# Two neighbouring rows of x per partition, and other row blocks of weights, in a sliding-window matmul that streams its weights

## Chip, cores, metric

One core of one Trainium2 chip. The metric is device time in microseconds, taken outside the profile; the span in a profile, from the first to the last instruction of the program, is some 2 us shorter (180.1 against 182.17 us in the kernel before).

## The reference

```python
B, S, D, W = 4, 4096, 4096, 64
x: (4, 4096, 4096) float32,  w: (4096, 4096) float32,  offsets: (4,) int64
for b in range(B):
    o = int(offsets[b])
    results.append(x[b, o:o+W] @ w)        # 64 rows of x against all of w
return np.stack(results)                   # (4, 64, 4096) float32
```

There are 256 rows of x in all, so w (67 MB) is read once and dominates the bytes.

## The kernel before

Weights come from HBM in float32 and are cast to fp16 by the DMA on the way (the profile has 71.3 MB read from HBM, while the DMA packets, as written and with the 4.19 MB of stores, are 40.97 MB). They arrive in row blocks of r k tiles: partition p holds rows p·r to p·r+r-1 of the block, so one piece of a transfer is r·16 KB long in HBM. The blocks live in a ring of three buffers, and a transfer into a buffer waits for the matmuls that read it (GpSimd waited 108.1 us in all for PE before it issued blocks). x is read at run-time offsets, 64 rows a batch, transposed on TensorE (PE) with an identity, and used as the stationary operand. Two groups g of 128 rows are formed.

```python
blocks = [(0, 1), (1, 1), (2, 4), (6, 4), (10, 4), (14, 4), (18, 4), (22, 3), (25, 2), (27, 1)]
x16 = [x_pool.tile([P, D], fp16, name=f"xrow{g}") for g in range(G)]     # one row a partition
...
nc.gpsimd.dma_start(out=w_one[1][:], in_=w[P : 2 * P, :])                # k tile 1, then x
make_identity(nc, identity[:])
for b in range(B):
    g, m = divmod(b, 2)
    o = nc.values_load(...)
    nc.gpsimd.dma_start(out=x16[g][m * WIN : (m + 1) * WIN, :], in_=x[b][bass.ds(o, WIN), :])
for k0, r in blocks[2:]:
    if free < r:
        t = wc_pool.tile([P, R_MAX * N], fp16, name="wc", tag="wc")      # ring of 3
        free = R_MAX
    ...
    nc.gpsimd.dma_start(out=t[:, base : base + r * N],
        in_=w[k0 * P : (k0 + r) * P, :].rearrange("(p r) n -> p (r n)", r=r))
...                                             # transposes of g = 0, then of g = 1
whole_rows([0, 1], True)                        # matmuls of 2 k tiles, copied to acc
for k0, r in blocks[2:-n_join]:
    whole_rows(range(k0, k0 + r))               # matmuls of a block, added to acc
...                                             # k 25 to 31 by column halves, with their stores
out_rows = out.rearrange("b m n -> (b m) n")
```

K tile 0 comes in float32 over the queue of SyncE and is cast by ScalarE. K tiles 28 to 31 (the tail) come in column pieces, so that the last half of the output can be finished soon after the last piece lands (landing at 169.33 us, PE's last matmul at 171.67). The first half of the output is stored from GpSimd's queue, the second from those of ScalarE and SyncE.

Of the kernel before, what the change touches and what calls it, by code (L numbers as in the profile page):

```python
# [10 lines left out]
def kernel(  # L11
# [7 lines left out]
    nc = tc.nc  # L19
    fp32 = mybir.dt.float32  # L20
    fp16 = mybir.dt.float16

    B, S, D = x.shape
    _, N = w.shape
    WIN = out.shape[1]
    P = 128
    NT = 512
    NG = N // 2
    n_k = D // P
    n_sub = NG // NT  # L30
    G = B // 2
    POOL = mybir.EngineType.Pool


    blocks = [(0, 1), (1, 1), (2, 4), (6, 4), (10, 4), (14, 4), (18, 4), (22, 3), (25, 2), (27, 1)]
    n_join = 2
    k_tail = 28
    n_fine = 2
# [3 lines left out]
    x_pool = ctx.enter_context(tc.tile_pool(name="xp", bufs=1))  # L42
    wc_pool = ctx.enter_context(tc.tile_pool(name="wc", bufs=3))
    w1_pool = ctx.enter_context(tc.tile_pool(name="w1", bufs=1))
# [2 lines left out]

    identity = const_pool.tile([P, P], fp16, name="identity")
    off_t = const_pool.tile([1, B], mybir.dt.int64, name="off_t")
    x16 = [x_pool.tile([P, D], fp16, name=f"xrow{g}") for g in range(G)]  # L50
    xT = [x_pool.tile([P, D], fp16, name=f"xT{g}") for g in range(G)]
    w_one = [w1_pool.tile([P, N], fp16, name=f"w1_{i}") for i in range(2)]
    tmp = [acc_pool.tile([P, 2 * NT], fp32, name=f"tmp{i}") for i in range(G)]
    acc = [acc_pool.tile([P, N], fp32, name=f"acc{g}") for g in range(G)]
    pairs = [psum_pool.tile([P, 2 * NT], fp32, name=f"banks{t}") for t in range(4)]

    def banks(b, n=1):
        return pairs[b // 2][:, b % 2 * NT : (b % 2 + n) * NT]
# [4 lines left out]
    w0_32 = acc[1]  # L63
    nc.sync.dma_start(out=w0_32[:, :NG], in_=w[0:P, :NG])
    nc.scalar.dma_start(out=off_t[:], in_=offsets[None, :])
    nc.sync.dma_start(out=w0_32[:, NG:], in_=w[0:P, NG:])
    nc.scalar.copy(out=w_one[0][:, :NG], in_=w0_32[:, :NG])  # L67
    nc.scalar.copy(out=w_one[0][:, NG:], in_=w0_32[:, NG:])  # L68
    off_i32 = off_t.bitcast(mybir.dt.int32)

    nc.gpsimd.dma_start(out=w_one[1][:], in_=w[P : 2 * P, :])  # L71
    make_identity(nc, identity[:])
    for b in range(B):
        g, m = divmod(b, 2)
        o = nc.values_load(  # L75
            off_i32[0:1, 2 * b : 2 * b + 1],
            engines=[POOL],
            min_val=0,
            max_val=S - WIN,
            skip_runtime_bounds_check_because="offsets are drawn below S - WIN",  # L80
        )
        nc.gpsimd.dma_start(  # L82
            out=x16[g][m * WIN : (m + 1) * WIN, :],
            in_=x[b][bass.ds(o, WIN), :],
        )


    src = {
        0: lambda a, e: w_one[0][:, a:e],
        1: lambda a, e: w_one[1][:, a:e],  # L90
    }
    free = 0
    for k0, r in blocks[2:]:
        if free < r:
            t = wc_pool.tile([P, R_MAX * N], fp16, name="wc", tag="wc")
            free = R_MAX
        base = (R_MAX - free) * N
        free -= r
        nc.gpsimd.dma_start(  # L99
            out=t[:, base : base + r * N],  # L100
            in_=w[k0 * P : (k0 + r) * P, :].rearrange("(p r) n -> p (r n)", r=r),
        )
        for q in range(r):
            src[k0 + q] = lambda a, e, t=t, c=base + q * N: t[:, c + a : c + e]


    tail = {}
# [5 lines left out]
    t = wc_pool.tile([P, R_MAX * N], fp16, name="wc", tag="wc")  # L113
    pos = 0
    for ng, st in zip(order, (steps, fine_steps)):
        for ki, n, c0, c1 in st:
            wd = c1 - c0
            nc.gpsimd.dma_start(  # L118
                out=t[:, pos : pos + n * wd].rearrange("p (t n) -> p t n", t=n),
                in_=w[ki * P : (ki + n) * P, ng * NG + c0 : ng * NG + c1].rearrange(  # L120
                    "(t p) n -> p t n", p=P
                ),
            )
            for q in range(n):
                for j in range(wd // NT):
                    a = pos + q * wd + j * NT
# [3 lines left out]
    def x_cols(g, kt):  # L130
        for k0, r in blocks:
            if k0 <= kt < k0 + r:
                a = k0 * P + kt - k0
                return x16[g][:, a : a + r * (P - 1) + 1 : r]
        return x16[g][:, kt * P : (kt + 1) * P]

    for g in range(G):
        for t in range(4):
            for i in range(8):
                nc.tensor.matmul(  # L140
                    out=pairs[t][:, i * P : (i + 1) * P],
                    lhsT=x_cols(g, 8 * t + i),
                    rhs=identity[:],
                    start=True,
                    stop=True,
                )
            dst = xT[g][:, 2 * t * NT : 2 * (t + 1) * NT]
            if t % 2 == 0:
                nc.vector.tensor_copy(out=dst, in_=pairs[t][:])  # L149
            else:  # L150
                nc.scalar.copy(out=dst, in_=pairs[t][:])  # L151

    def mm(bank, g, kt, rhs, start, stop):
        nc.tensor.matmul(  # L154
            out=banks(bank),
            lhsT=xT[g][:, kt * P : (kt + 1) * P],
            rhs=rhs,
            start=start,
            stop=stop,
        )  # L160

    def add_out(bank, n, g, c):
        dst = acc[g][:, c * NT : (c + n) * NT]
        nc.vector.tensor_add(out=dst, in0=dst, in1=banks(bank, n))  # L164
# [3 lines left out]
    def whole_rows(kts, first=False):  # L168
        nonlocal n_pair
        for g in range(G):  # L170
            for c in range(0, 2 * n_sub, 2):
                b0 = n_pair % 4 * 2
                n_pair += 1
                for j in range(2):
                    for i, kt in enumerate(kts):
                        rhs = src[kt]((c + j) * NT, (c + j + 1) * NT)
                        mm(b0 + j, g, kt, rhs, i == 0, i == len(kts) - 1)
                dst = acc[g][:, c * NT : (c + 2) * NT]
                if not first:
                    add_out(b0, 2, g, c)  # L180
                elif c % 4 == 0:
                    nc.vector.tensor_copy(out=dst, in_=banks(b0, 2))  # L182
                else:
                    nc.scalar.copy(out=dst, in_=banks(b0, 2))  # L184

    whole_rows([0, 1], True)
    for k0, r in blocks[2:-n_join]:
        whole_rows(range(k0, k0 + r))
    join = range(blocks[-n_join][0], k_tail)
# [3 lines left out]
        rhs = src[ki](c * NT, (c + 1) * NT) if ki < k_tail else tail[(ki, c)]  # L193
        mm(4 * g + j, g, ki, rhs, start, stop)

    out_rows = out.rearrange("b m n -> (b m) n")

    def store(eng, g, c0, c1, cuts=(0, P)):
        for a, e in zip(cuts, cuts[1:]):
            eng.dma_start(out=out_rows[g * P + a : g * P + e, c0:c1], in_=acc[g][a:e, c0:c1])  # L200

    def columns(ng, kts):
        for ki in kts:
# [14 lines left out]
    for g in range(G):  # L218
        store(nc.gpsimd, g, ng * NG, (ng + 1) * NG)
# [8 lines left out]
    for h in range(2):  # L228
        js = range(h * n_sub // 2, (h + 1) * n_sub // 2)
        for ki in range(k_fine, n_k):  # L230
            for g in range(G):
                for j in js:
                    tail_mm(ki, g, ng, j, False, ki == n_k - 1)
        for g in range(G):
            add_out(4 * g + js[0], 2, g, ng * n_sub + js[0])
            c0 = ng * NG + h * NG // 2
            store(q[g], g, c0, c0 + NG // 2)
# [30 lines left out]
```

## Time and profile before

| | before |
|---|---|
| median of 3 runs | 182.17 us (182.05 to 182.88) |
| span in the profile | 180.1 us |
| PE busy | 128.2 us, 71% |
| DMA queues, share of 16 engines | 100% |
| read from HBM / written | 71.3 / 4.19 MB |

How to read it: PE is TensorE's matmuls and PEld its loads of the stationary operand, DVE is VectorE, ACT is ScalarE, POOL is GpSimd; a transfer "lands" when the trace reports its end. The digits of a row in the 40 slices are tenths of a slice of 4.5 us in which that engine was busy. The DMA share is the mean over 16 engines. A stretch's share can pass 1 a little (1.16 from 13.3 to 23.1 us), as the query books a piece's time whole where it starts. The rows themselves stand in the prediction.

### The profile page before, as it was taken

To read this page: it belongs to the slowest core of one execution; us is meant where nothing else is said; L and a number is where in the kernel's file an instruction comes from. 1 tells how busy PE (TensorE), PEld (TensorE's weight loads), DVE (VectorE), ACT (ScalarE), POOL (GpSimd) and SP (SyncE) were. 2 spreads that over 40 slices of the span, in tenths; PEclk is the share of its full clock that TensorE was granted. 3 is DMA by queue.
4 is the path that set the end of the run, shared out by engine and by line. 5 is a ranking of instruction groups with operands and counts; after the bars stand their busy time and mean duration, and the time that the engine had idled before them with its cause. 6 is when DMAs were issued, how large, how long until landed. Compare 5 with 4: busy or idle time off the path is not lost.

```text
span 180.1 us, 1403 instructions
## 1 busy us (share of the span) xinstructions
PE 128.2 (71%) x576; PEld 57.3 (32%) x576; DVE 82.2 (46%) x68; ACT 16.9 (9%) x15; POOL 12.7 (7%) x27
## 2 busy tenths in 40 slices
PE   0000789104999499938996599949999999999910
PEld 0000764001344134413442134414444444443400
DVE  0000566200276427642566036733778975407560
ACT  2422346200000000000000000000000004004000
POOL 4600000000000100010001000020007100000200
PEclk9999999855599969996999569987999999999995
DMA  5999979999998899999989999999999999999996
GB/s 187 313 260 213 286 160 211 236 233 226 233 233 175 182 233 233 236 218 233 204 175 218 233 233 220 222 193 202 229 206 215 198 211 213 214 214 207 338 412 241
DMA packets 4151, 40.97 MB, mean 227 GB/s; under 512 B 434, under 2 KB 434, under 8 KB 2226
## 3 DMA queue, kind: packets, MB, share of 16 engines
q0 software_dynamic: 3280, 36.70, 93.5%
q1 hardware_dynamic: 576, 3.15, 4.6%
q10 hardware_dynamic: 290, 1.05, 1.5%
q8 instruction: 4, 0.07, 0.1%
q14 instruction: 1, 0.01, 0.0%
HBM read 71.30 MB, written 4.19 MB: 419 GB/s over the span
## 4 chain that ended last, share of the span: by engine, by line
DMA 43%; PE 43%; issue 4%; DVE 2%; another core or an unknown queue 1%; POOLq 1%; DVEq 1%; POOL 1%
DMA wc<-in_w_dram 43%; PE banks L154 43%; DVE acc L164 2%; DVEq L263 1%; POOLq L75 1%; POOL xrow L82 0%; POOL identity masks.py:197 0%; POOLq L82 0%; POOL w L71 0%; POOLq masks.py:199 0%; DVEq L164 0%; POOLq L252 0%
## 5 line engine op out<-in xcount | busy, mean ns | idle before, releaser
L154 PE MATMUL banks<-wc,xT 128*128 128x512 f16 x480 | 115.8, 405 | 23.6 <-DMA wc<-in_w_dram 23.3
L164 DVE TENSOR_TENSOR acc<-acc,banks 128x1024 f32<-128x1024 f32 x56 | 67.9, 1221 | 69.0 <-PE banks L154 68.4
L154 PEld LDWEIGHTS <-xT 128*128 128x128 f16 x512 | 52.3, 103 | 93.9 <-DMA wc<-in_w_dram 26.4
L140 PE MATMUL banks<-identity,xrow 128*128 128x128 f16 x64 | 5.3, 261 | 19.9 <-DMA xrow<-in_x_dram 19.9
L209 ACT COPY tmp<-banks 128x1024 f32<-128x1024 f32 x4 | 3.9, 1016 | 128.2 <-PE banks L154 128.2
L149 DVE CAST xT<-banks 128x1024 f16<-128x1024 f32 x4 | 4.8, 1222 | 21.5 <-PE banks L140 21.5
L99 POOL DMA_DIRECT2D wc<-in_w_dram x8 | 4.3, 539 | 108.1 <-PE banks L154 108.1
L140 PEld LDWEIGHTS <-xrow 128*128 128x128 f16 x64 | 5.1, 127 | 20.0 <-issue 20.0
L154 PE MATMUL banks<-w,xT 128*128 128x512 f16 x32 | 7.1, 379 | 0.0
L182 DVE COPY acc<-banks 128x1024 f32<-128x1024 f32 x4 | 4.9, 1225 | 1.6 <-PE banks L154 1.6
L118 POOL DMA_DIRECT2D wc<-in_w_dram x6 | 3.9, 674 | 17.1 <-PE banks L154 17.1
L213 DVE TENSOR_TENSOR acc<-acc,tmp 128x1024 f32<-128x1024 f32 x4 | 4.7, 1218 | 0.0
L151 ACT CAST xT<-banks 128x1024 f16<-128x1024 f32 x4 | 4.0, 1014 | 7.9 <-PE banks L140 7.9
L184 ACT COPY acc<-banks 128x1024 f32<-128x1024 f32 x4 | 4.0, 1012 | 3.0 <-PE banks L154 3.0
L200 POOL DMA_DIRECT2D out_dram<-acc x2 | 1.1, 537 | 27.2 <-DVE acc L213 27.2
L68 ACT CAST w<-acc 128x2048 f16<-128x2048 f32 x1 | 1.9, 1898 | 4.8 <-DMA acc<-in_w_dram 4.8
L82 POOL DMA_DIRECT2D xrow<-in_x_dram x4 | 2.1, 524 | 2.1 <-issue 2.1
L67 ACT CAST w<-acc 128x2048 f16<-128x2048 f32 x1 | 1.9, 1898 | 3.1 <-DMA acc<-in_w_dram 3.1
L67 ACT ACT_TABLE_LOAD x1 | 1.3, 1283 | 1.4 <-PEq L252 1.4
L71 POOL DMA_DIRECT2D w<-in_w_dram x1 | 0.7, 660 | 0.8 <-POOLq L252 0.8
masks.py:199 POOL TENSOR_SCALAR_AFFINE_SELECT identity<-identity 128x128 f16<-128x128 f16 x1 | 0.3, 287 | 0.1
masks.py:197 POOL MEMSET identity<- 128x128 f16 x1 | 0.2, 223 | 0.0
(4 smaller groups left out, 0.4 us busy)
## 6 DMA issues: line engine op xcount, KB each, us to landing
wc<-in_w_dram POOLq DMA_DIRECT2D x5, 4096.0 KB, 42.1
wc<-in_w_dram POOLq DMA_DIRECT2D x4, 1024.0 KB, 24.5
wc<-in_w_dram POOLq DMA_DIRECT2D x1, 3072.0 KB, 37.1
acc<-in_w_dram SPq DMA_DIRECT2D x2, 1024.0 KB, 8.1
xrow<-in_x_dram POOLq DMA_DIRECT2D x4, 512.0 KB, 14.4
wc<-in_w_dram POOLq DMA_DIRECT2D x1, 2048.0 KB, 26.4
out_dram<-acc POOLq DMA_DIRECT2D x2, 1024.0 KB, 5.6
w<-in_w_dram POOLq DMA_DIRECT2D x1, 1024.0 KB, 11.8
```

The lines of the kernel that those rows point to most:

```text
L67: nc.scalar.copy(out=w_one[0][:, :NG], in_=w0_32[:, :NG])
L99: nc.gpsimd.dma_start(out=t[:, base : base + r * N], in_=w[k0 * P : (k0 + r) * P, :].rearrange("(p r) n -> p (r n)", r=r),)
L118: nc.gpsimd.dma_start(out=t[:, pos : pos + n * wd].rearrange("p (t n) -> p t n", t=n), in_=w[ki * P : (ki + n) * P, ng * NG + c0 : ng * NG ...
L140: nc.tensor.matmul(out=pairs[t][:, i * P : (i + 1) * P], lhsT=x_cols(g, 8 * t + i), rhs=identity[:], start=True, stop=True,)
L149: nc.vector.tensor_copy(out=dst, in_=pairs[t][:])
L151: nc.scalar.copy(out=dst, in_=pairs[t][:])
L154: nc.tensor.matmul(out=banks(bank), lhsT=xT[g][:, kt * P : (kt + 1) * P], rhs=rhs, start=start, stop=stop,)
L164: nc.vector.tensor_add(out=dst, in0=dst, in1=banks(bank, n))
L182: nc.vector.tensor_copy(out=dst, in_=banks(b0, 2))
L184: nc.scalar.copy(out=dst, in_=banks(b0, 2))
L209: nc.scalar.copy(out=tmp[g][:], in_=banks(4 * g + 2, 2))
L213: nc.vector.tensor_add(out=dst, in0=dst, in1=tmp[g][:])
```

## The change

The intent, as far as the code tells: longer pieces for x (two neighbouring rows, 32 KB instead of 16), no block of one k tile at the head of the queue, and equal or smaller blocks towards the end. Group g now holds the rows of parity g, so the output rows are interleaved to match. The block of 2 lives in the ring and stands ahead of x in the queue.

```diff
-    blocks = [(0, 1), (1, 1), (2, 4), (6, 4), (10, 4), (14, 4), (18, 4), (22, 3), (25, 2), (27, 1)]
+    blocks = [(0, 1), (1, 2), (3, 4), (7, 4), (11, 4), (15, 4), (19, 3), (22, 3), (25, 2), (27, 1)]
-    x16 = [x_pool.tile([P, D], fp16, name=f"xrow{g}") for g in range(G)]
+    x16 = x_pool.tile([P, G * D], fp16, name="xrow")
-    w_one = [w1_pool.tile([P, N], fp16, name=f"w1_{i}") for i in range(2)]
+    w_one = w1_pool.tile([P, N], fp16, name="w1")
...
-    nc.gpsimd.dma_start(out=w_one[1][:], in_=w[P : 2 * P, :])
+    load_block(*blocks[1])
     make_identity(nc, identity[:])
...
-            out=x16[g][m * WIN : (m + 1) * WIN, :],
-            in_=x[b][bass.ds(o, WIN), :],
+            out=x16[b * PB : (b + 1) * PB, :],
+            in_=x[b][bass.ds(o, WIN), :].rearrange("(p g) d -> p (g d)", g=G),
...
-                return x16[g][:, a : a + r * (P - 1) + 1 : r]
+                return x16[:, g * D + a : g * D + a + r * (P - 1) + 1 : r]
...
-    whole_rows([0, 1], True)
+    whole_rows(range(0, 3), True)
...
-    out_rows = out.rearrange("b m n -> (b m) n")
+    out_rows = out.rearrange("b m n -> (b m) n").rearrange("(p g) n -> g p n", g=G)
...
-            eng.dma_start(out=out_rows[g * P + a : g * P + e, c0:c1], in_=acc[g][a:e, c0:c1])
+            eng.dma_start(out=out_rows[g, a:e, c0:c1], in_=acc[g][a:e, c0:c1])
```

## The prediction

> **What bounds the kernel now.** I read the page first: engine shares, the 40 slices and the HBM line, to see who is full.
>
> ```profile
> PE 128.2 (71%) x576; PEld 57.3 (32%) x576; DVE 82.2 (46%) x68; ACT 16.9 (9%) x15; POOL 12.7 (7%) x27
> ...
> PE   0000789104999499938996599949999999999910
> ...
> DMA  5999979999998899999989999999999999999996
> ...
> HBM read 71.30 MB, written 4.19 MB: 419 GB/s over the span
> ...
> DMA 43%; PE 43%; issue 4%; DVE 2%; another core or an unknown queue 1%; POOLq 1%; DVEq 1%; POOL 1%
> ```
>
> The DMA row is full from the first slice to the last; PE has holes until slice 24. The chain of waits (last line) gives PE as much as DMA, so it can't decide alone. Next I looked at stretches cut at the landings of the weight blocks (columns: length, busy time and count of PE, PEld, DVE, ACT, POOL, granted clock, DMA share, GB/s as written).
>
> ```profile
> 13.30:23.10 9.80, 3.40 (x32) 3.26 (x32) 2.45 (x2) 3.16 (x3) 0.00 (x0) 1.00 1.16 243
> 23.20:43.00 19.80, 8.99 (x64) 4.89 (x64) 7.24 (x6) 5.97 (x6) 0.00 (x0) 0.80 0.99 213
> ...
> 81.70:101.00 19.30, 15.67 (x64) 6.62 (x64) 9.77 (x8) 0.00 (x0) 0.53 (x1) 0.88 1.01 217
> 101.00:120.30 19.30, 16.73 (x64) 6.90 (x64) 9.77 (x8) 0.00 (x0) 1.06 (x2) 0.85 0.98 212
> 120.50:134.80 14.30, 14.30 (x59) 6.12 (x60) 7.75 (x7) 0.00 (x0) 0.00 (x0) 0.88 1.02 219
> 134.90:144.50 9.60, 9.60 (x46) 4.34 (x45) 8.65 (x8) 0.00 (x0) 3.92 (x6) 1.00 0.96 204
> 144.60:149.40 4.80, 4.78 (x23) 2.08 (x22) 2.94 (x3) 0.00 (x0) 0.00 (x0) 1.00 0.99 205
> ...
> 169.30:178.30 9.00, 2.37 (x11) 0.87 (x9) 4.62 (x4) 0.00 (x0) 0.00 (x0) 0.82 0.99 403
> ```
>
> The reader is to see a DMA share of about 1 in every stretch, whatever PE does. A block of 4 k tiles takes 19.3 us to arrive and PE needs 15.7 to 16.7 us for it. GB/s counts fp16 written; each byte is two read, so 217 means 434 GB/s from HBM. Last I read the waits of the tail and the timeline there:
>
> ```profile
> PE banks L154 <- DMA wc<-in_w_dram: 2.6, 1, 2.6
> ...
> 78.30 0.53 POOL L99 DMA_DIRECT2D wc<-in_w_dram  x1 [17.65 <-PE banks L154]
> ...
> 118.17 1.06 POOL L99 DMA_DIRECT2D wc<-in_w_dram  x2 [19.91 <-PE banks L154]
> 120.44 51.23 PE L154 MATMUL banks<-wc,xT 128*128 128x512 f16 x224 [2.57 <-DMA wc<-in_w_dram]
> ```
>
> POOL's long waits for PE (108 us in total) are for a free weight buffer, and they cost nothing: the transfer issued at 78.30 lands at 120.4 (42.1 us to landing) although its own bytes need 19.3 us, so the queue still held 22 us of work when it was issued. PE is without a gap from 120.44 to 171.67, yet the DMA engines are also full until 178. So the bound is the sum of bytes and pieces over 16 DMA engines, from 1.9 us to about 178.5 us, plus some 1.5 us of completion.
>
> [...]
> 1. [...] 4 tiles are 8.39 MB read in 19.3 us, 435 GB/s. [...]
> 2. [...] the four x pieces land 12.2, 13.7, 15.2 and 16.8 us after issues at 3.54, 4.48, 5.42 and 6.35, so at 15.7, 18.2, 20.6 and 23.15, every 2.44 us; 1.05 MB read in 2.44 us is 430 GB/s[...].
> 3. [...] The transfer writes fp16, at half the read rate (215 GB/s), which the 64-partition form sustains today.
> 4. [...] The output's pitch goes from 16 to 32 KB[...]. No stretch of this trace has that pitch.
>
> **The change part by part.**
>
> Pieces of x. Removed: 4 transfers of 64 pieces of 16 KB (8 KB written). Added: 4 of 32 pieces of 32 KB, the same bytes. Before: 4 x 2.44 = 9.76 us. A 32 KB piece is known from the weight block of 2 tiles: its 128 pieces land 26.4 us after 118.17 (144.54, the median view gives 26.4) and the block ahead, issued at 97.73, lands 37.1 us later, at 134.85; 9.69 us for 8 pieces per engine, 1.21 us each. x then needs 4 x 2 x 1.21 = 9.69 us. Saving 0.07 us. It is this small because a piece costs about its bytes: half of a 1.21 us piece is 0.605, against 0.61 for the small one.
>
> Row blocks. Both lists have nine queued blocks and 27 tiles; a 1 and a 4 become a 2 and a 3. Before: 4.93 + 19.3 = 24.2 us (the last single tile lands at 149.47, 4.93 after 144.54). After: 9.69 + 14.46 (the block of 3, 120.39 to 134.85) = 24.15. Saving 0.08 us. Byte total unchanged: 71.3 MB read.
>
> Order of arrival. Two tiles now stand ahead of x, so x lands complete at 23.15 + 4.8 = about 28 us, and all transposes wait for all four x transfers, where half of them began at 18.3. Transposes 3.4 + 1.95 us of PE plus the copies: first weight matmul at about 33.4 us instead of 25.2. Then 3 tiles = 48 matmuls at 0.22 = 10.6 us, to 44 us. The next block (k 3 to 6) lands at 43.03 + 4.8 = 47.8, so PE is again early, by 3.8 us instead of 10.8. This 8 us delay is hidden.
>
> Buffers. The block of 2 now lives in the 3-buffer ring; the first reuse (k 11 to 14) waits for the matmuls of k 1 and 2, done at 44, while queued work lasts until k 7 to 10 lands at about 67: 23 us to spare. The next reuses are issued at about 64 (queue until 86), 83 (until 106), 102 (until 120), 122 (until 135), and the tail at about 133 (until 149; before: 136.4). The smallest reserve is 13 us, where before it was 13.1 (136.4 to 149.5). DMA never starves.
>
> Tail. At 120.4 us PE has 3 tiles queued instead of 4: it needs 48 x 0.23 = 11 us after finishing k 15 to 18 at 122, so 133, waits 1.7 us for k 22 to 24 at 134.7, and runs about 1.4 us ahead of before. But at 164.3 PE's weight load already waited for a DMA, and the last weight piece lands at 169.3 in either version. After it 4.19 MB of stores remain, at 403 to 425 GB/s some 9.9 us: 169.2 + 9.9 = 179.1. The four stores of the last half are issued up to 1.4 us sooner into a full queue: 0 to 0.4 us from a better filled end.
>
> Casts, adds, matmul counts: equal (576 matmuls, seven rounds of adds or copies).
>
> Sum: 182.17 - 0.07 - 0.08 - about 0.05 for the end = 181.97, say 181.95 us.
>
> **Rivals.**
> (a) The tail is PE's. For: the chain of waits runs through PE from 120.4 on, and PE has no gap. Then the 1.4 us that PE gains would show: 180.8 us. Against: DMA is full from 169 to 178 with stores.
> (b) The late start of PE reaches the end. For: first matmul 8 us later. Against: PE still waits for k 3 to 6, and every later block gives 3 us back. If a buffer were released late and the queue ran dry for 3 us: 185.
> (c) 32-partition transfers spread badly[...]. x at half speed would cost 9.7 us: 192, outside 2%. [...]
> (d) Interleaved output rows (4 or 8 KB pieces at 32 KB pitch) write slower. A tenth on 9.9 us of stores is 1 us: 183.1. For it I have no trace[...].
>
> **Range and chances.** Before's runs spread over 182.05 to 182.88, so 0.8 us is noise. The computed gain of 0.2 us is under that. (a) pulls down, (d) up, both by at most 1.3 us. I take 181.3 to 182.7 for 8 in 10. 2% is 3.6 us: (c) alone or a starved queue gets there, 1.5%; a gain of 3.6 us has no source while the bytes stay, 1%.
>
> **What would show it.** x transfers: four landings 2.4 us apart, the last near 28 us; twice as far apart would mean (c). First weight matmul near 33 us, PE's wait for k 3 to 6 about 4 us. DMA share near 1 in all stretches, last weight landing at 169.0 to 169.4. PE's total wait for weights falls from 23.3 us to about 15. A PE gap of 1 to 2 us near 133. Stores over 169 to 179 at 400 GB/s; lower would mean (d). A DMA row with a slice under 9 in the middle would make the prediction wrong.

182.17 - 0.07 - 0.08 - about 0.05 us is 181.97, said as 181.95. That 32 pieces of x would spread over 16 engines like 64, two to an engine, stands behind the 0.07 us and was all that spoke against rival (c); before the change no trace showed it, so it, and the small chance given to (c), were the author's estimate. What spoke against rival (d) was not shown either. x_alone tests both. Of the other figures, 0.22 us for a matmul is 32 in 7.07 us (from 25.2 us on), 0.23 is 224 in 51.23 us, the 403 to 425 GB/s of stores is an estimate (403 is the last stretch, and its whole microseconds read 401 to 422), and the 0.05 us for the end is a guess inside the 0 to 0.4 us named there.

## The result

The changed kernel takes 182.14 us, median of 6 runs (182.02 to 182.25), against 182.44 us for the kernel before in the same rounds (6 runs, 181.90 to 182.88). The ratio is 0.9985 with a 95% interval of 0.9964 to 1.0007: the same. A ratio here is the mean time of one kernel's fast runs over that of the other's of the same rounds, so it is not quite the ratio of the two medians.

From the page of the changed kernel (slices, HBM bytes, chain of waits by line):

```profile
PE   0000006999499919993799949999939998998900
...
DMA  5999998999998999999999999999999999999995
...
HBM read 71.30 MB, written 4.19 MB: 419 GB/s over the span
...
DMA wc<-in_w_dram 63%; PE banks L157 26%; DVE acc L167 1%; POOL wc L121 1%; DVEq L266 1%; POOLq L95 1%; POOL xrow L102 0%; POOL identity masks.py:197 0%; POOLq L102 0%; POOL wc L83 0%; POOLq masks.py:199 0%; DVEq L167 0%; POOLq L255 0%
```

The DMA row is as full as before and the bytes are the same. PE starts two slices later. The chain of waits has moved from half PE to mostly DMA: not because DMA does more, but because PE now waits for weights late in the run, so that the walk back from the last instruction crosses to the DMA at 164.5 us instead of at 120.4. That the chain changes its owner while the span stays (180.1 and 180.3 us) I read as two limits that end almost together: in both kernels PE's last matmul ends 2.1 to 2.3 us after the last landing of weights.

The same stretches as before, cut at the landings of the changed kernel (length, then busy time and count of PE, PEld, DVE, ACT, POOL, granted clock, DMA share, GB/s written): x, the block k 3 to 6, the block k 11 to 14, the block k 22 to 24, the end.

```profile
18.40:28.40 10.00, 0.00 (x0) 0.00 (x0) 0.00 (x0) 0.47 (x1) 0.00 (x0) 1.00 1.09 231
28.40:47.80 19.40, 16.66 (x112) 10.77 (x112) 9.79 (x8) 8.10 (x8) 0.53 (x1) 1.00 1.01 217
67.10:86.60 19.50, 15.67 (x64) 6.58 (x64) 9.77 (x8) 0.00 (x0) 0.53 (x1) 0.88 1.00 216
...
120.50:134.90 14.40, 11.35 (x53) 4.92 (x51) 11.51 (x10) 0.00 (x0) 3.81 (x6) 1.00 1.01 216
...
169.30:178.30 9.00, 2.35 (x11) 0.88 (x9) 4.61 (x4) 0.00 (x0) 0.00 (x0) 0.76 0.98 399
```

Every stretch is as full as before (DMA share 0.98 to 1.09), and a block of 4 still takes 19.3 to 19.5 us. The stores run at 399 GB/s, against 403. In the stretch from 120.5 PE is busy for 11.35 of 14.40 us, where it was busy throughout before. The timeline of PE in the tail shows where the rest is:

```profile
117.66 14.19 PE L157 MATMUL banks<-wc,xT 128*128 128x512 f16 x65
134.97 14.16 PE L157 MATMUL banks<-wc,xT 128*128 128x512 f16 x64 [3.12 <-DMA wc<-in_w_dram]
149.57 14.42 PE L157 MATMUL banks<-wc,xT 128*128 128x512 f16 x64 [0.44 <-DMA wc<-in_w_dram]
164.57 7.08 PE L157 MATMUL banks<-wc,xT 128*128 128x512 f16 x32 [0.58 <-DMA wc<-in_w_dram]
```

PE waits 3.1 us ahead of the tail, then hands the rest of its lead back in two waits for weights (0.44 and 0.58 us), and ends at 171.65 us, as before (171.67). Last landing of weights: 169.53 us (before 169.33).

### The profile page after: what moved, and what is told of

It is laid out like the page before. It is cut to its first block, busy times and chain, and to the rows that moved or that the text cites. A ratio compares the mean times of both kernels' runs of the same rounds, so it can differ in the third digit from the quotient of the medians.

```text
span 180.3 us, 1404 instructions
## 1 busy us (share of the span) xinstructions
PE 125.8 (70%) x576; PEld 57.5 (32%) x576; DVE 82.2 (46%) x68; ACT 17.0 (9%) x15; POOL 12.6 (7%) x27
## 4 chain that ended last, share of the span: by engine, by line
DMA 63%; PE 26%; issue 3%; POOL 1%; DVE 1%; POOLq 1%; DVEq 1%
DMA wc<-in_w_dram 63%; PE banks L157 26%; DVE acc L167 1%; POOL wc L121 1%; DVEq L266 1%; POOLq L95 1%; POOL xrow L102 0%; POOL identity masks.py:197 0%; POOLq L102 0%; POOL wc L83 0%; POOLq masks.py:199 0%; DVEq L167 0%; POOLq L255 0%
## 5 line engine op out<-in xcount | busy, mean ns | idle before, releaser
L157 PE MATMUL banks<-wc,xT 128*128 128x512 f16 x496 | 118.7, 397 | 17.2 <-DMA wc<-in_w_dram 17.1
L157 PEld LDWEIGHTS <-xT 128*128 128x128 f16 x512 | 51.3, 101 | 85.2 <-DMA wc<-in_w_dram 19.6
L143 PE MATMUL banks<-identity,xrow 128*128 128x128 f16 x64 | 6.3, 294 | 28.6 <-DMA xrow<-in_x_dram 28.6
L143 PEld LDWEIGHTS <-xrow 128*128 128x128 f16 x64 | 6.2, 140 | 28.5 <-issue 28.5
L83 POOL DMA_DIRECT2D wc<-in_w_dram x9 | 4.9, 549 | 112.6 <-PE banks L157 111.8
L157 PE MATMUL banks<-w,xT 128*128 128x512 f16 x16 | 6.1, 379 | 0.0
L121 POOL DMA_DIRECT2D wc<-in_w_dram x6 | 3.9, 677 | 9.3 <-PE banks L157 9.3
## 6 DMA issues: line engine op xcount, KB each, us to landing
xrow<-in_x_dram POOLq DMA_DIRECT2D x4, 512.0 KB, 19.5
```

The costliest lines, as they stand in the source:

```text
L83: nc.gpsimd.dma_start(out=t[:, base : base + r * N], in_=w[k0 * P : (k0 + r) * P, :].rearrange("(p r) n -> p (r n)", r=r),)
L121: nc.gpsimd.dma_start(out=t[:, pos : pos + n * wd].rearrange("p (t n) -> p t n", t=n), in_=w[ki * P : (ki + n) * P, ng * NG + c0 : ng * NG ...
L143: nc.tensor.matmul(out=pairs[t][:, i * P : (i + 1) * P], lhsT=x_cols(g, 8 * t + i), rhs=identity[:], start=True, stop=True,)
L157: nc.tensor.matmul(out=banks(bank), lhsT=xT[g][:, kt * P : (kt + 1) * P], rhs=rhs, start=start, stop=stop,)
```

## The experiments

Two questions were tested. The first is the prediction's: does the sum of DMA work set the end, with PE's lead or lag hidden? The rival is that PE's gapless tail sets it. The second came up with the result: the kernel before has two groups of times, the changed one doesn't. 46 timed runs of the kernel before fall into 27 between 181.70 and 182.17 us and 19 between 182.40 and 182.93.

### The changed kernel again (after_again)

No edit.

> The changed kernel once more, for the spread of both kernels on one chip. Theory: ratio 0.997 to 1.001. If the small gain of the first measurement (0.9985) came from before's three runs at 182.7 to 182.9, and those are part of before's nature, before shows two groups again, 182.0 and 182.8, and the changed kernel only the lower one.

Measured: 182.08 us (6 runs, 182.01 to 182.29), before 182.06 us (11 runs, 181.73 to 182.93); ratio 0.9993, 0.9965 to 1.0020. As expected, before shows both groups (5 of 11 above 182.5) and the changed kernel none of the upper. It isn't as fast as before's lower group, though: its mean is 182.13, that of the six lower runs 181.83. So the ratio near 1 is a mixture of two things of opposite sign, both under 0.5%.

### x alone (x_alone)

The kernel before with only the rows of x and of the output changed (the diff is cut to the load of x; the tiles, the transposes and the output rows follow it):

```diff
-            out=x16[g][m * WIN : (m + 1) * WIN, :],
-            in_=x[b][bass.ds(o, WIN), :],
+            out=x16[b * PB : (b + 1) * PB, :],
+            in_=x[b][bass.ds(o, WIN), :].rearrange("(p g) d -> p (g d)", g=G),
```

> Only the form of x and of the output rows is changed; the blocks stay 1,1,4,4,4,4,4,3,2,1. Theory (the 16 DMA engines are full, and x's bytes are the same): ratio to before 0.997 to 1.001, x's four landings about 2.4 us apart, stores at the end again about 400 GB/s. Rival (c), 32-partition transfers spread badly: landings 4.8 us apart, 190 us. Rival (d), output rows at 32 KB pitch write slower: stretch of stores below 370 GB/s, 183 us or more.

Measured: 182.16 us (181.99 to 182.61), ratio 0.9993, 0.9965 to 1.0022. The four parts of x land at 16.1, 18.45, 21.1 and 23.5 us, 2.4 to 2.6 us apart. So these transfers to 32 partitions were served about as fast as those to 64 before, which landed 2.44 us apart, and rival (c) falls. The stretch of the stores, 169.3 to 178.3 us, reads:

```profile
169.30:178.30 9.00, 3.47 (x17) 1.37 (x14) 4.62 (x4) 0.00 (x0) 0.32 (x1) 0.93 1.01 406
```

406 GB/s at 32 KB row pitch against 403 at 16 KB: rival (d) falls too. From the landing of k tile 1 to the last of x it is 9.90 us, against 9.94 before: the predicted saving of 0.07 us can't be told from nothing.

### Row blocks alone (blocks_alone)

The changed kernel with x and the output as before (the diff is cut in the same way):

```diff
-            out=x16[b * PB : (b + 1) * PB, :],
-            in_=x[b][bass.ds(o, WIN), :].rearrange("(p g) d -> p (g d)", g=G),
+            out=x16[g][m * WIN : (m + 1) * WIN, :],
+            in_=x[b][bass.ds(o, WIN), :],
```

> Only the row blocks are changed (1,2,4,4,4,4,3,3,2,1, the block of 2 in the ring, x behind it); x and output as before. Theory: ratio 0.997 to 1.001, first weight matmul near 33 us, a gap of about 3 us on PE before k 22 to 24, last weight landing within 0.3 us of before's 169.33. Rival (a), the tail is PE's: 1 to 1.5 us faster than before, 0.993.

Measured: 182.58 us (182.26 to 183.41), ratio 1.0018, 0.9986 to 1.0051. Not faster, so rival (a) has no support. It is slower than the whole change (medians 182.58 and 182.08 on the same chip). In its trace PE waits 3.76 us before k 22 to 24, the clock then falls to half from 135.9 us for 3.4 us, and PE ends at 172.8 us instead of 171.7. Two later experiments take this up.

### One k tile less to read (one_tile_less)

The changed kernel without the load of k tile 2 (its matmuls read tile 1's weights, in a line that is cut here):

```diff
+        n_got = 1 if k0 == 1 else r
-            out=t[:, base : base + r * N],
-            in_=w[k0 * P : (k0 + r) * P, :].rearrange("(p r) n -> p (r n)", r=r),
+            out=t[:, base : base + n_got * N],
+            in_=w[k0 * P : (k0 + r) * P, :].rearrange("(p r) n -> p (r n)", r=r)[:, : n_got * N],
```

> The changed kernel without the load of k tile 2: its matmuls read tile 1's weights again, so the result is wrong on purpose and PE's work is the same; 2.1 MB less are read, early in the run. Theory (DMA is the sum): 4.8 to 5.0 us faster, 177.3 us, ratio 0.973. Rival (a), PE sets the end: under 1.5 us faster. Rival of fixed latencies at the start: nearly nothing.

Measured: 177.32 us (4 runs, 177.19 to 177.90; result wrong), ratio 0.9736, 0.9699 to 0.9773. All engines do the same work, 2.1 MB less are read, and 4.76 us are gone, against after_again on the same chip. The last weights land at 164.6 us, 4.8 to 4.9 us sooner. The time follows the bytes. Alone this doesn't decide against rival (a): PE's last matmul ends as much sooner, at 166.7 us, and PE waits for weights seven times in this run (19.0 us in all), so that it may end sooner only because they land sooner. It is the next run, with the same bytes and less work for PE, that decides.

### Less work for PE in the tail (before_less_pe)

The kernel before without the matmuls of k tile 24, whose weights are still loaded:

```diff
-        whole_rows(range(k0, k0 + r))
+        whole_rows(range(k0, k0 + r - (k0 == 22)))
```

> The kernel before without the 16 matmuls of k tile 24 (result wrong on purpose; its weights are still loaded): 3.4 us less of PE in the stretch where PE has no gap, 120 to 172 us. Theory (DMA is the sum): ratio 0.996 to 1.001. Rival (a), the tail is PE's: 2.5 to 3.4 us faster, 0.983.

Measured: 182.01 us (4 runs, 181.93 to 182.05; result wrong) against 182.09, ratio 0.9985, 0.9954 to 1.0015. Taking 16 matmuls from PE's tail (3.4 us, by what 16 added ones cost in before_late_pe: PE's end at 175.1 instead of 171.7 us) doesn't move the lower group. Rival (a) falls for the lower group: a faster PE gains nothing there. All four runs are of that group; four are few, but with the rest below they fit.

### Later PE, in both kernels (before_late_pe, after_late_pe)

The first matmul of each bank is done twice in the block ahead of the tail, k 18 to 21 of the kernel before and k 19 to 21 of the changed one (the number in the condition is 18 and 19):

```diff
                 for j in range(2):
+                    if kts[0] == 18:
+                        mm(b0 + j, g, kts[0], src[kts[0]]((c + j) * NT, (c + j + 1) * NT), True, True)
                     for i, kt in enumerate(kts):
```

> The kernel before with the first matmul of each bank in block k 18 to 21 done twice (right result): 16 more matmuls, 3.4 us of PE just ahead of the gapless tail. PE then ends about 2.8 us later (0.6 us of its lag was a wait at 164 us), the last store is issued at about 177 instead of 174.2. Theory: the four stores then no longer all queue behind one another; 0.7 to 2 us slower, ratio 1.004 to 1.011. Rival (DMA alone counts, whatever PE does): 1.000.

> The same 16 more matmuls in the changed kernel, in block k 19 to 21. Theory: PE's gap of 3.1 us before k 22 takes them up; ratio to before 0.997 to 1.002, the gap falls under 0.5 us. Rival (the change gave PE no usable reserve): as slow as the same addition to the kernel before.

Measured: before_late_pe 186.15 us (6 runs, 184.92 to 186.55), ratio 1.0215, 1.0183 to 1.0247 (slower clear of noise; against the 2% limit the verdict is unclear). after_late_pe 182.16 us (4 runs, 181.81 to 182.48), ratio 0.9992, 0.9957 to 1.0026. The changed kernel takes the 3.4 us up in its gap, as expected: PE is busy for all of 11 us there (window 126 to 137 us). The kernel before loses far more than the 0.7 to 2 us that I had expected, and this is a miss. The first store's issue of before_late_pe (timeline) and the DMA row of its last 23 us (slices from 160 to 183 us) show what I had not counted:

```profile
170.26 0.54 POOL L202 DMA_DIRECT2D out_dram<-acc  x1 [26.56 <-DVE acc L215]
```

```profile
DMA  9999999999999621000599899999999999999600
```

The last weights have landed at 169.5 us, but the first store is issued only at 170.3, because it too hangs on PE. So the DMA engines stand idle for about 3 us between loads and stores (the low slices). In this profiled run PE ends 3.4 us later and the span is 3.0 us longer. The median run is 1.2 us slower still than the profiled one; no trace tells why.

So the kernel before is at a balance: less work for PE gains nothing, and 3.4 us more cost 3.0 us in the profiled run and 4.1 us by median. The changed kernel has about 3 us in hand there.

### Small pieces (small_pieces)

The changed kernel, each row block of weights loaded one row per partition at a time:

```diff
-        nc.gpsimd.dma_start(
-            out=t[:, base : base + r * N],
-            in_=w[k0 * P : (k0 + r) * P, :].rearrange("(p r) n -> p (r n)", r=r),
-        )
+        for q in range(r):
+            nc.gpsimd.dma_start(
+                out=t[:, base + q * N : base + (q + 1) * N],
+                in_=w[k0 * P : (k0 + r) * P, :].rearrange("(p r) n -> p (r n)", r=r)[:, q * N : (q + 1) * N],
+            )
```

> The changed kernel with each row block of weights loaded one row per partition at a time: pieces of 16 KB read instead of 32, 48 or 64 KB, same bytes, same places, 26 transfers instead of 9. It shows what piece size is worth if all of it is used. Theory: a tile in 16 KB pieces took 4.93 us, one in 64 KB pieces 4.83, so 26 tiles cost 1.5 to 3 us more, 184 us, ratio 1.01. Rival (pieces are free): 0.998 to 1.003. Rival (issue or semaphores of 26 transfers starve the queue): slices of DMA under 9 and over 186 us.

Measured: 182.86 us (4 runs, 182.77 to 183.72), ratio 1.0047, 1.0007 to 1.0086, 0.8 us over before. The interval lies just above 1, and the difference is half of the least that was expected (27 transfers, by count in the trace, not 26). The last row block lands at 150.26 us against 149.53: 0.73 us for 27 tiles' worth of transfers, 0.03 us a tile. Four tiles take 19.47 us in 16 KB pieces, and 19.3 to 19.5 in 64 KB pieces. My 4.93 us for a single tile was read off one landing and was too long for a mean. The whole lever of piece size, 16 KB against the 32 to 64 KB of these 27 tiles, is worth 0.4%. The change moves it for 2 tiles' worth of x and one block.

### Where the two groups of the kernel before come from (before_trace1, before_trace2, before_warm, blocks_alone_warm)

The traces pointed to PE's granted clock: after a wait for weights it often falls to half, in steps of 3.4 us. In the clock records of the 14 traces only 1.0 and 0.5 occur, and the half-clock stretches ahead of PE's end last 3.4, 6.8, 10.2 or 13.7 us, after waits of 2.3 to 11 us. The length of the wait alone doesn't tell what follows: the 2.52 us up to 62.3 us in the kernel before are followed by 3.4 us at half clock, the 3.12 us up to 135.0 us in the changed kernel are not. The end of this section comes back to it.

The first two runs are the kernel before once more, without an edit, for further traces.

> The kernel before, unchanged, for a second trace. Theory: a run above 182.4 us shows 6.8 us at half clock at about 120 us (or a later dip) and PE's last matmul near 172.7; a run below 182.2 shows 3.4 us there and 171.7. Rival: the same PE end in both, and later landings of weights.

> The kernel before, unchanged, for a third trace, with the same expectation as the second: above 182.4 us a dip of 6.8 us and a last matmul near 172.7, below 182.2 a dip of 3.4 us and 171.7.

Measured: 181.91 us and 182.84 us (single runs, state unknown), by luck one of each group. Here is the stretch from 120 to 127 us, after the last long wait of PE, in before_trace1 and then in before_trace2; the number after the busy times is the granted clock.

```profile
120.00:127.00 7.00, 6.58 (x24) 2.70 (x25) 2.44 (x2) 0.00 (x0) 0.00 (x0) 0.76 1.05 225
```

```profile
120.00:127.00 7.00, 6.51 (x17) 2.40 (x18) 1.22 (x1) 0.00 (x0) 0.00 (x0) 0.54 1.03 221
```

PE is "busy" equally long in both, but gets 24 matmuls done in one and 17 in the other: 7 fewer at 0.22 us (64 in 14.16 us in the changed kernel's tail above) are 1.5 us of work lost. The clock records put the half-clock stretch at 3.4 us in the first and 6.8 us in the second. PE's last matmul ends at 171.4 and 173.0 us; the last weights land at 169.3 and 169.1, so DMA is not the cause. A third trace fits: x_alone has the same blocks and tail, and its profiled run (182.61 us) shows 6.8 us at half clock from 119.0 us and PE's end at 172.8. The timeline of the tail:

```profile
120.42 43.65 PE L154 MATMUL banks<-wc,xT 128*128 128x512 f16 x192 [2.79 <-DMA wc<-in_w_dram]
164.31 7.11 PE L154 MATMUL banks<-wc,xT 128*128 128x512 f16 x32 [0.24 <-DMA wc<-in_w_dram]
```

```profile
120.48 52.51 PE L154 MATMUL banks<-wc,xT 128*128 128x512 f16 x224 [5.32 <-DMA wc<-in_w_dram]
```

The first is before_trace1, where PE still has to wait for weights at 164.3 us; the second is before_trace2, where PE is the later one to the end. The two runs differ earlier already: before_trace1 has 6.8 us at half clock at 99.4 us and then waits 2.79 us, before_trace2 has none there and waits 5.32 us. To turn this from an observation into a test, PE was kept busy through the wait by matmuls whose result is overwritten:

```diff
         whole_rows(range(k0, k0 + r))
+        if k0 == 14:
+            for i in range(12):
+                mm(n_pair % 4 * 2, i % G, k0, src[k0](0, NT), True, True)
```

> The kernel before with 12 more matmuls (2.6 us, on data that are there, overwritten afterwards, right result) between blocks k 14 to 17 and k 18 to 21, where PE waits 2.6 to 3.8 us for weights. In the traces so far the clock then falls to half for 3.4 or 6.8 us, which is 1.7 or 3.4 us of PE work lost just ahead of the gapless tail. Theory (the spread of before, 181.7 to 182.1 and 182.5 to 182.9, is how long that dip lasts): clock 1.00 from 112 us on, PE's last matmul ends at 171.5 or sooner, no run in the upper group, ratio 0.996 to 1.000. Rival (the spread comes from DMA or elsewhere): two groups remain. Rival (the additional matmuls only delay PE): as slow as before_late_pe in proportion, 184 us.

Measured: 181.95 us (6 runs, 181.76 to 182.23) against 182.09 (11 runs, 181.79 to 182.83, five of them above 182.5); ratio 0.9982, 0.9957 to 1.0007. No run falls in the upper group; if 27 of 46 runs fall in the lower one, six of six would do so by chance in 4% of cases. The same stretch now has the full clock and 30 matmuls:

```profile
120.00:127.00 7.00, 6.44 (x30) 2.93 (x30) 3.50 (x3) 0.00 (x0) 0.88 (x2) 1.00 1.01 218
```

Of the kernels with a right result this one has the lowest median and the lowest ratio, and its interval still reaches 1; it can't be called faster.

The same was done to blocks_alone, in its 3.76 us wait (after the block k 19 to 21, the condition being `k0 == 19`):

> The new row blocks with x as before (182.26 to 183.41 us in six runs, where the whole change has 182.01 to 182.29), plus 12 more matmuls (2.6 us, overwritten afterwards, right result) after block k 19 to 21, where its trace shows PE waiting 3.8 us and then 3.4 us at half clock from 135.9 us. Theory: the clock stays at 1.00 from there on, PE's last matmul ends near 171.5 instead of 172.8, all runs between 181.8 and 182.4, ratio to before 0.996 to 1.000. Rival (the old form of x itself costs with the new blocks, in DMA): runs stay above 182.3 on average.

Measured: 182.18 us (6 runs, 182.01 to 182.47), ratio 1.0005, 0.9985 to 1.0024; the clock stays at 1.00 from 109.4 us on and PE ends at 171.5. One run is a little over the expected 182.4. The slow runs of blocks_alone, up to 183.41, are gone. That speaks for a dip of the clock and against the old form of x as such; it is six runs on another chip, and of the slow runs only one (183.14) was traced.

The clock records of all 14 traces say more than the account so far uses. Their edges lie whole multiples of 3.413 us apart. Cut each trace at these edges, from the first record to PE's last matmul, and set the share of a window in which PE is idle against the clock of the next window. Of 497 windows at full clock, all 437 with up to 58% idle are followed by full clock and all 57 with 61% or more by half; the three between went both ways. Of 91 windows at half clock, all 58 with up to 23% idle are followed by full clock, all 33 with 24% or more by half. So in these traces it is not the length of a wait alone that counts but how the edges cut it. Four windows, from the changed kernel, blocks_alone, before_trace1 and before_trace2:

```profile
132.96:136.37 3.41, 1.40 (x7) 0.69 (x8) 0.15 (x1) 0.00 (x0) 3.12 (x5) 1.00 1.02 216
```

```profile
132.52:135.93 3.41, 0.62 (x3) 0.31 (x4) 0.29 (x1) 0.00 (x0) 3.09 (x6) 1.00 0.94 199
```

```profile
119.91:123.32 3.41, 2.90 (x7) 1.03 (x8) 0.00 (x0) 0.00 (x0) 0.00 (x0) 0.50 1.04 223
```

```profile
119.62:123.03 3.41, 2.54 (x7) 0.90 (x8) 0.00 (x0) 0.00 (x0) 0.00 (x0) 0.50 1.04 223
```

In the changed kernel an edge divides the 3.1 us wait: 32% of one window is idle and 59% of the next, and the clock stays (in after_again 42 and 43%). In blocks_alone 82% of one window is idle and the clock falls; in small_pieces a wait of only 2.27 us takes 66% of a window, and it falls too. In before_trace1 the window at half clock is 15% idle and the clock comes back after 3.4 us; in before_trace2 it is 25% idle, and a second window follows at half. This was worked out afterwards and no run was made to test it; what sets the place of the edges in a run isn't shown.

## Why the prediction was right

The time (182.14 against 181.95 predicted, inside the range) and the verdict of "same" hold, in the main for the reason given. That the median lies below before's of the same rounds is luck: three of before's six runs fell in its upper group. Against its lower group the changed kernel is 0.1 us slower in those rounds, so the predicted gain of 0.2 us isn't seen. Step by step:

- **The bound is the DMA sum.** Shown by two runs together: a tile less is 4.76 us less (one_tile_less), 3.4 us less of PE is nothing (before_less_pe). The trace shows a read rate of 435 GB/s (8.39 MB in 19.3 us), written as fp16 at 217 GB/s in the same stretch, and not which part sets it.
- **x pieces, 0.07 us saved.** Transfers as fast as before: shown (x_alone, 2.4 to 2.6 us apart against 2.44). The saving itself: not resolved. In the changed kernel x takes 10.07 us from the landing of the block ahead (18.35 to 28.42 us), before 9.94. My 9.76 left out that in the kernel before the first of the four landings was 2.52 us after the block ahead.
- **Blocks, 0.08 us saved.** Not seen: k 24 has landed at 134.92 us, before at 134.85. The single tile was mis-sized at 4.93 us; small_pieces gives 4.87 (2.1 MB read in 16 KB pieces, 431 GB/s).
- **Order of arrival.** x complete at 28.4 (predicted 28), first weight matmul at 34.7 (33.4; all 64 transposes ran slowly, 6.3 us instead of 5.35), PE's wait for k 3 to 6 2.6 us (3.8). PE's whole wait for weights 17.1 us (15). Hidden, as said.
- **Buffers.** The DMA row has no hole. The tail's transfers are issued at 132.2 us, predicted 133.
- **Tail.** A gap of 3.1 us before k 22 to 24 was seen where 1.7 was predicted, since PE ended that block at 131.9 and not 133. PE's end unmoved: the lead is given back in waits at 149.6 and 164.6 us, which I had named as the reason why (a) wouldn't count. The 0.05 us gain at the end isn't to be seen.

What the prediction lacked: it took before's spread of 0.8 us for noise. In the traces it is a dip of PE's clock of 3.4 or 6.8 us at the start of a tail that has no reserve. And it argued the tail in one direction only. "DMA is full from 169 to 178" holds if PE is sooner; if PE is later, the stores that fill those microseconds aren't there yet (before_late_pe).

Still open: the changed kernel is 0.1 to 0.3 us behind before's lower group on the same chips, and no trace shows a stage where this arises. None of its 12 runs is in an upper group, but only two of them were traced: in both the edges of the clock windows divide the 3 us wait, and whether that holds for the other ten isn't known.

## What to carry to other kernels

When all DMA engines are full from the first load to the last store, as here, count bytes first: 2.1 MB less were worth 4.76 us. Rearranging the same bytes into longer or shorter pieces was worth under half a per cent (small_pieces, ratio 1.0047). Then ask what happens if the other engine is late, not only if it is early; the kernel before, in which both end together, had no reserve (3.4 us more of PE cost 3.0 us in the profiled run), and a clock dip of 6.8 us instead of 3.4 came through as 0.9 us between two traces. Two groups of times in one kernel are worth a second trace of each before they are called noise.
